# A decoder step's state-space mixer: value products of two attention steps in one run, the skip term on ScalarE, the decays' logs of a group loaded ahead

## The chip, the core and the metric

The kernel runs on one core of a Trainium2 chip. The metric is the time of one execution on the device in microseconds (us), the median of three runs. A profile of one execution is read beside it. TensorE (PE in the profile) does the matrix products, VectorE (DVE) and ScalarE (ACT) the elementwise work, GpSimd (POOL) some additions, and SyncE (SP) issues most transfers.

## What is computed

One layer of a hybrid decoder for 256 prompt positions and 8 sample rows of width 2048, all in float32. The part that matters here is the first sub-layer: one input projection, whose columns are split among a sliding-window attention (16 query heads, 4 key heads, window 128) and a Mamba-2 state-space mixer (32 heads in 4 groups, chunks of 128 positions).

```python
proj = rms_norm(x, w['g_mix']) @ w['w_in']
q, k, v, z, xbc, dt_raw = jnp.split(proj, IN_SPLITS, axis=-1)
# attention over the window: logits, softmax with a sink, then
o = jnp.einsum('bnkgqs,bnskd->bnqkgd', p.astype(v.dtype), vv)
# mixer, after a causal convolution and SiLU of x, B and C:
la = jnp.cumsum(dt * a, axis=2)                       # per head and chunk
decay = jnp.exp(jnp.where(causal, la[:, :, :, None] - la[:, :, None, :], -jnp.inf))
y = jnp.einsum('bclsgh,bcsghp->bclghp', cb[..., None] * decay, xdt)
y = y + jnp.einsum('bclgn,bcghpn->bclghp', cm, h_prev) * jnp.exp(la)[..., None]
y = y + xs * d_skip                                   # the skip term
y = rms_norm(y * silu(z), norm_g)
x = x + jnp.concatenate([attn, ssd], axis=-1) @ w['w_out']
```

Cross-attention and a convolutional feed-forward network follow. The sample rows take one step of the same formulas from states in memory: their y needs, for each head, the stored state h0 times C, summed.

## The kernel before

**Projections.** A weight arrives in parts of 128 x 1024 (`wraw`, line 83, SP's queue). ScalarE rounds it to a high half (`whi`, L89), VectorE makes the low half from the rest (`wlo`, L90), and TensorE multiplies: three matmuls for each 128x128 block (L104 to L106: high times high, high times low of the activations, low times high), 24 for a part, 264 columns each. There are four buffers each of wraw, whi and wlo. An input pair (`in_pair`) is four parts and ends in two accumulators that VectorE takes out of PSUM.

**The order of the work.** A scheduler sets each engine's order while the program is built; a name that stands in `tc.issue_after(...)` keeps an instruction behind another one, and weights have high priority. Each engine then runs its list strictly in order. So small matmuls of the attention and the mixer lie between the projections' matmuls where the scheduler put them.

**Attention.** `attn_first(j)` does the first 128 queries of two query blocks j and j+1, `attn_prompt(j, ..., 1)` the second 128 of one block: logits, softmax on VectorE and ScalarE, transposes of the probabilities into PSUM, a copy to `pt`, and then four value matmuls of 64 output rows each, L602 in the one and L564 in the other. The norms of q come from eight matmuls with 32 output rows (L620), two for each of four column groups. `attn_sample` does the sample rows.

**Mixer.** `la`, the cumulative logs, comes from a product with a triangle of ones (L479, L480); a turned copy of it is computed by two more matmuls (L482) and written to memory as `dram_la`. `ssd_prompt(g)` works on group g in two chunks: it loads the logs of four heads at a time, broadcast to all partitions, into tiles `e` (L810; three buffers shared with `kl` of the attention), turns them into decays (L814, L815 on ScalarE), multiplies with C times B (L816 on VectorE), multiplies with x dt on TensorE (L830, eight matmuls of 64 rows), and adds the skip term on VectorE, four instructions (L833). The carried state's part needs `ti`, loaded by L841. `ssd_sample(g)` loads half of the group's C rows (`cb`, L870, GpSimd's queue) and a quarter of a state (`h0`, L873), and VectorE multiplies and sums (L874, L875). `conv_pair` and `z_pair` take two accumulators out into separate tiles `u` of a ring of four.

The stage's order in the program is: `conv_group` 0 and 1, `ssd_prompt(0)`, `conv_group(2)`, `ssd_sample(0)`, `ssd_prompt(1)`, `conv_group(3)`, and then the z pairs with the other groups between them.

Of the kernel before, what the change touches and what calls it, by code (L numbers as in the profile page):

```python
# [7 lines left out]
F32 = mybir.dt.float32  # L8
F32R = mybir.dt.float32r
AF = mybir.ActivationFunctionType  # L10
ALU = mybir.AluOpType
# [37 lines left out]
def hybrid_decoder_step_kernel(ctx: ExitStack, tc: tile.TileContext, I, O):  # L49
# [26 lines left out]
    def weights(src, n=2048, into=None):  # L76

        out = []
        with tc.high_priority():
            for o in range(0, n, NPART):  # L80
                w = min(NPART, n - o)
                x = raw_part(w)
                nc.sync.dma_start(out=x, in_=src[:, o:o + w])
# [397 lines left out]
    for c in range(2):  # L481
        PE.matmul(p[0:32, 128 + c * 128:256 + c * 128], dtan[:, c, :], tri, start=True, stop=True)  # L482
# [11 lines left out]
    for i in range(4):  # L494
        u = mp.tile([128, 3 + T], F32, name=f"u{i}")
        P.memset(u[:, 0:3], 0.0)
        ring.append(u)
    ringn = [0]

    def next_u():  # L500
        ringn[0] += 1
        return ring[ringn[0] % 4]

    laT = next_u()[0:32, 3:259]
    V.tensor_copy(out=laT, in_=p[0:32, 128:384])
    nc.sync.dma_start(out=dram_la.rearrange("c h l -> h c l"), in_=laT.rearrange("p (c l) -> p c l", c=2))
# [18 lines left out]
    def attn_prompt(j, rq, nrq, c):  # L525
# [33 lines left out]
        pt = mp.tile([128, 4, 128], F32, tag="bc", name="pt", bufs=2)  # L559
        S.copy(out=pt[:, 0:2 * nb, :], in_=p[:, 0:2 * nk].rearrange("p (a q) -> p a q", q=128))  # L560
        o = psum("t")
        for h in range(2):
            for kb in range(nb):
                PE.matmul(o[64 * h:64 * h + 64, 0:128], vn[:, kb, pp, 64 * h:64 * h + 64], pt[:, h * nb + kb, :],  # L564
                          start=kb == 0, stop=kb == nb - 1)
        marks["attn"] = S.copy(out=attn[:, j, c * 128:c * 128 + 128], in_=o[:, 0:128])

    def attn_first(j):
# [29 lines left out]
        S.copy(out=pt, in_=p.rearrange("p (a q) -> p a q", q=128))  # L598
        o = psum("t")
        for i in range(4):  # L600
            h = i % 2
            PE.matmul(o[64 * h:64 * h + 64, 128 * (i // 2):128 * (i // 2) + 128], vn[:, 0, pp, 64 * h:64 * h + 64], pt[:, i, :], start=True, stop=True)  # L602
        S.copy(out=attn[:, j:j + 2, 0:128], in_=o[:, 0:256].rearrange("p (i q) -> p i q", i=2))
# [14 lines left out]
    for d in range(2):  # L618
        for j in range(4):
            PE.matmul(pq[32 * j:32 * j + 32, 0:TP], nw[:, d, :], qsq[d][:, j, :TP], start=d == 0, stop=d == 1)  # L620
# [42 lines left out]
    for j in range(0, 8, 2):  # L663
        attn_first(j)
# [934 lines left out]
```

## Time and profile before

| what | value |
|---|---|
| median of three runs | 1382.97 us (1382.23 to 1383.33) |
| the profiled execution | 1382.65 us, span 1380.6 us |
| TensorE busy | 1375.4 us, weight loads 1348.0 us |
| VectorE, ScalarE, GpSimd busy | 1050.0, 765.8, 96.1 us |
| L602, 16 matmuls in 32 records | 2.6 us busy |
| L564, 32 matmuls in 64 records | 5.3 us busy |
| L620, 8 matmuls in 16 records | 2.3 us busy |
| L482, 2 matmuls in 4 records | 0.6 us busy |
| L830, 64 matmuls in 128 records | 9.0 us busy |

A float32 matmul is two records in the profile, a projection's matmul and a transpose are one. Records of TensorE overlap, so what a matmul costs is read from start to start. The mixer and attention stage lies between about 40 and 410 us of the span; the projections go on through all of it.

### The profile page before, as it was taken

Reading aid. Unit: us, or ns where it says so; the run is one execution under the profiler, and the core shown is the slowest. Engines: PE = TensorE matmul, PEld = TensorE weight load, DVE = VectorE, ACT = ScalarE, POOL = GpSimd, SP = SyncE. Lnnn points to the kernel's source line nnn. Section 1 sums busy time; section 2 is a strip of 40 time slices with the busy share of each in tenths; the row PEclk is TensorE's granted clock in tenths of the full one; section 3 lists DMA queues with packets and bytes.
Section 4 is the critical chain, followed back from the end, with each engine's and each line's share of the span. In section 5 each row is a group of like instructions: output and inputs, shape, how many; then the busy total and the mean of one; then the engine's idle time right before and its main releaser. Section 6 shows DMA issues by size and latency. Waiting matters only on the chain.

```text
span 1380.6 us, 28767 instructions
## 1 busy us (share of the span) xinstructions
PE 1375.4 (100%) x11415; PEld 1348.0 (98%) x11415; DVE 1050.0 (76%) x1865; ACT 765.8 (55%) x1261; POOL 96.1 (7%) x286
## 2 busy tenths in 40 slices
PE   9999999999999999999999999999999999999999
PEld 8999999999999999899999999999999999999998
DVE  7979799999987784579777765776577657765655
ACT  7667756556545555566565544554455445543532
POOL 0000011111000000002010000000000000000000
PEclk9999999999999999999999999999999999999999
DMA  7954468777677576865676766676567656656554
GB/s 297 333 161 134 147 209 254 228 247 256 227 230 240 185 232 213 303 235 198 190 260 214 257 215 186 212 260 213 185 214 244 198 183 198 198 183 185 193 186 139
DMA packets 89478, 298.32 MB, mean 216 GB/s; under 512 B 12032, under 2 KB 17152, under 8 KB 88832
## 3 DMA queue, kind: packets, MB, share of 16 engines
q1 hardware_dynamic: 83840, 277.61, 60.5%
q0 software_dynamic: 5504, 18.88, 4.2%
q8 instruction: 89, 1.46, 0.4%
q14 instruction: 45, 0.37, 0.1%
HBM read 280.77 MB, written 16.23 MB: 215 GB/s over the span
## 4 chain that ended last, share of the span: by engine, by line
PE 99%; DMA 0%; ACT 0%; SPq 0%; DVE 0%; issue 0%
PE mm L106 21%; PE mm L104 21%; PE mm L105 21%; PE t L106 10%; PE t L104 10%; PE t L105 10%; PE t L245 1%; PE t L283 1%; PE y L830 1%; PE y L846 0%; PE x L283 0%; DMA open<-in_open_dram 0%; PE s L245 0%; PE mm L245 0%; PE t L564 0%; PE x L1144 0%
## 5 line engine op out<-in xcount | busy, mean ns | idle before, releaser
L89 ACT CAST whi<-wraw 128x1024 fp32r<-128x1024 f32 x440 | 459.9, 1047 | 518.3 <-PE mm L105 270.2
L90 DVE TENSOR_TENSOR wlo<-wraw,whi 128x1024 fp32r<-128x1024 f32 x440 | 541.7, 1232 | 216.4 <-ACT whi L89 210.2
L106 PE MATMUL t<-x2h,wlo 128*128 128x264 f32 x704 | 198.5, 282 | 0.0
L104 PE MATMUL t<-x2h,whi 128*128 128x264 f32 x704 | 198.4, 282 | 0.0
L105 PE MATMUL t<-x2l,whi 128*128 128x264 f32 x704 | 198.4, 282 | 0.0
L105 PE MATMUL mm<-hl,whi 128*128 128x264 f32 x704 | 197.5, 282 | 0.0
L106 PE MATMUL mm<-hh,wlo 128*128 128x264 f32 x704 | 197.2, 282 | 0.0
L104 PE MATMUL mm<-hh,whi 128*128 128x264 f32 x704 | 195.7, 282 | 0.0
L104 PE MATMUL mm<-x2h,whi 128*128 128x264 f32 x672 | 189.3, 282 | 0.0
L105 PE MATMUL mm<-x2l,whi 128*128 128x264 f32 x672 | 189.3, 282 | 0.0
L106 PE MATMUL mm<-x2h,wlo 128*128 128x264 f32 x672 | 189.3, 282 | 0.0
L104 PE MATMUL mm<-xh,whi 128*128 128x264 f32 x576 | 163.7, 285 | 0.0
L105 PE MATMUL mm<-xl,whi 128*128 128x264 f32 x576 | 163.4, 285 | 0.0
L106 PE MATMUL mm<-xh,wlo 128*128 128x264 f32 x576 | 162.3, 286 | 0.0
L104 PEld LDWEIGHTS t<-x2h,whi 128*128 128x128 f32 x704 | 131.9, 187 | 0.0
L106 PEld LDWEIGHTS t<-x2h,wlo 128*128 128x128 f32 x704 | 131.9, 187 | 0.0
L105 PEld LDWEIGHTS t<-x2l,whi 128*128 128x128 f32 x704 | 131.9, 187 | 0.0
L105 PEld LDWEIGHTS mm<-hl,whi 128*128 128x128 f32 x704 | 131.9, 187 | 0.0
L106 PEld LDWEIGHTS mm<-hh,wlo 128*128 128x128 f32 x704 | 131.7, 187 | 0.0
L104 PEld LDWEIGHTS mm<-hh,whi 128*128 128x128 f32 x704 | 130.8, 187 | 0.0
L104 PEld LDWEIGHTS mm<-x2h,whi 128*128 128x128 f32 x672 | 125.9, 187 | 0.0
L105 PEld LDWEIGHTS mm<-x2l,whi 128*128 128x128 f32 x672 | 125.9, 187 | 0.0
(518 smaller groups left out, 2939.5 us busy)
## 6 DMA issues: line engine op xcount, KB each, us to landing
wraw<-in_w_up_dram SPq DMA_DIRECT2D x176, 512.0 KB, 4.2
wraw<-in_w_in_dram SPq DMA_DIRECT2D x96, 512.0 KB, 4.7
wraw<-in_w_dn_dram SPq DMA_DIRECT2D x88, 512.0 KB, 4.3
wraw<-in_w_out_dram SPq DMA_DIRECT2D x48, 512.0 KB, 4.3
h<-in_h_dram POOLq DMA_DIRECT2D x32, 256.0 KB, 4.6
hn<-in_h_dram SPq DMA_DIRECT2D x16, 512.0 KB, 4.9
out_state_s_dram<-hn POOLq DMA_DIRECT2D x16, 512.0 KB, 3.5
e<-dram_la SPq DMA_DIRECT2D x16, 256.0 KB, 4.4
```

The source lines that it names most:

```text
L89: S.copy(out=hi, in_=x)
L90: V.tensor_tensor(out=lo, in0=x, in1=hi.bitcast(F32), op=ALU.subtract)
L104: PE.matmul(out, wh, xh, start=start, stop=False)
L105: PE.matmul(out, wh, xl, start=False, stop=False)
L106: return PE.matmul(out, wl, xh, start=False, stop=stop)
L245: PE.matmul(first[c][:, :T], pre[k // 2][i][:, k % 2, c * 128:(c + 1) * 128], A[k // 8][x][:, k % 8, :], start=k + i + x == 0, stop=k == K ...
L283: return PE.transpose(out, in_, cst[0:k, C_ID:C_ID + k])
L830: PE.matmul(y[o:o + 64, (h // 2) * 128:(h // 2) * 128 + 128], xdt[:, h, :], es[h // 4][:, h % 4, :], start=True, stop=True)
```

## The change

Seven edits, all in the mixer and attention stage.

1. The value matmuls of two steps are issued in one run: `first_values` and `second_values` take the probabilities of two steps, the newer one's first matmul goes first, and the others are held behind it. Their copy out of PSUM is one instruction for both. A second pair of tiles for `pt` comes from the tags `hp` and `cb`.
2. The eight q-norm matmuls go in one run, behind the one whose input comes last.
3. The turned logs are one transpose of `la`, and `dram_la` is written from 64 rows.
4. The logs of a whole group (both chunks and `ti`) are loaded by `logs()` into one tile `late` with the tag `B`, that is, into the buffers that the attention's tiles (keys, values, zeros) had; the first two groups' loads stand ahead of `conv_group(1)`, the others behind a weight load. The product with C times B is one instruction for eight heads.
5. The skip term: ScalarE scales x by d_skip in place, four instructions, and VectorE adds y in one.
6. Pairs: `conv_pair` and `z_pair` use one tile `u` for both accumulators, so that copies, the tanh and the products of z are one instruction for two.
7. `ssd_sample` loads the group's C rows in one transfer; `ssd_sample(0)` stands ahead of `conv_group(1)`. Two small tiles of `attn_sample` move from the tag `h0` to `hp`.

```diff
-    for c in range(2):
-        PE.matmul(p[0:32, 128 + c * 128:256 + c * 128], dtan[:, c, :], tri, start=True, stop=True)
...
-    for i in range(4):
-        u = mp.tile([128, 3 + T], F32, name=f"u{i}")
+    for i in range(2):
+        u = mp.tile([128, 2, 3 + T], F32, name=f"u{i}")
...
+    p = psum("x")
+    tr(p[0:64, 0:128], la)
+    V.tensor_copy(out=laT, in_=p[0:64, 0:128])
+    nc.sync.dma_start(out=dram_la.rearrange("c h l -> (c h) l"), in_=laT)
...
-        o = psum("t")
-        for h in range(2):
-            for kb in range(nb):
-                PE.matmul(o[64 * h:64 * h + 64, 0:128], vn[:, kb, pp, 64 * h:64 * h + 64], pt[:, h * nb + kb, :],
-                          start=kb == 0, stop=kb == nb - 1)
-        marks["attn"] = S.copy(out=attn[:, j, c * 128:c * 128 + 128], in_=o[:, 0:128])
+        return pt
+
+    def second_values(j, pts):
+        pp = j // 4
+        o = psum("t")
+
+        def value(a, h, kb):
+            return PE.matmul(o[64 * h:64 * h + 64, 128 * a:128 * a + 128], vn[:, kb, pp, 64 * h:64 * h + 64], pts[a][:, 2 * h + kb, :],
+                             start=kb == 0, stop=kb == 1)
+
+        with tc.issue_after(value(1, 0, 0).ins):
+            for x in [(a, h, kb) for a in (1, 0) for h in range(2) for kb in range(2)][1:]:
+                value(*x)
+        marks["attn"] = S.copy(out=attn[:, j:j + 2, 128:TP], in_=o[:, 0:256].rearrange("p (i q) -> p i q", i=2))
...
-    for d in range(2):
-        for j in range(4):
-            PE.matmul(pq[32 * j:32 * j + 32, 0:TP], nw[:, d, :], qsq[d][:, j, :TP], start=d == 0, stop=d == 1)
+    with tc.issue_after(q_sums(1, 3).ins):
+        for d in (1, 0):
+            for j in range(4):
+                if (d, j) != (1, 3):
+                    q_sums(d, j)
...
+    def logs():
+
+        g = len(lates)
+        w = apool.tile([128, 8 * PITCH], F32, tag="B", name="late", bufs=4)
+        for c in range(2):
+            nc.sync.dma_start(out=w[:, 1024 * c:1024 * c + 1024].rearrange("p (h l) -> p h l", h=8),
+                              in_=dram_la[c, 8 * g:8 * g + 8, :].partition_broadcast(128))
+        ti = w[:, 2048:2560].rearrange("p (i l) -> p i l", i=4)
+        for h in range(2):
+            nc.sync.dma_start(out=ti[h * 64:h * 64 + 64], in_=lav[h][4 * g:4 * g + 4, :].partition_broadcast(64))
+        lates.append(w)
...
-            for i in range(4):
-                V.scalar_tensor_tensor(out=x[:, i, :], in0=x[:, i, :], scalar=pc("d_skip", 4 * g + i), in1=y[:, i * 128:i * 128 + 128],
-                                       op0=ALU.mult, op1=ALU.add)
+            for i in range(4):
+                S.activation(out=x[:, i, :], in_=x[:, i, :], func=AF.Copy, scale=pc("d_skip", 4 * g + i))
+            V.tensor_tensor(out=x, in0=x, in1=y.rearrange("p (i l) -> p i l", i=4), op=ALU.add)
...
+        cb = mp.tile([128, 8, 128], F32, tag="cb", name="cb", bufs=1)
+        nc.gpsimd.dma_start(out=cb, in_=dram_bc[1][8 * g:8 * g + 8, :].partition_broadcast(128))
...
     conv_group(0)
+    ssd_sample(0)
+    logs()
+    logs()
     conv_group(1)
     ssd_prompt(0)
     conv_group(2)
-    ssd_sample(0)
+    with tc.issue_after(marks["load"].ins):
+        logs()
     ssd_prompt(1)
     conv_group(3)
+    with tc.issue_after(marks["load"].ins):
+        logs()
```

Three places show how the engines' lists change. On TensorE, where the logs are made and q's squares are summed, it was (L104 to L106 are projections, L620 the sums):

```order
L104 MATMUL mm<-xh_77,whi 128x264
L479 MATMUL x<-dtan,cst 128x64
L480 MATMUL x<-dtan,cst 128x64
L482 MATMUL x<-cst,dtan 32x128 x2
L105 MATMUL mm<-xl_78,whi 128x264
L106 MATMUL mm<-xh_77,wlo 128x264
L104 MATMUL mm<-xh_77,whi 128x264
L105 MATMUL mm<-xl_78,whi 128x264
L106 MATMUL mm<-xh_77,wlo 128x264
L620 MATMUL s<-qsq_677,zz 32x256 x4
L620 MATMUL s<-qsq_678,zz 32x256 x2
```

and later two lone matmuls of L620. Now L479 and L480 stand alone, and some 36 projections later comes this (L637 is the new line of the sums):

```order
L106 MATMUL mm<-xh_75,wlo 128x264
L104 MATMUL mm<-xh_75,whi 128x264
L283 MATMUL x<-cst,la 64x128
L105 MATMUL mm<-xl_76,whi 128x264
L637 MATMUL s<-qsq_674,zz 32x256 x4
L637 MATMUL s<-qsq_673,zz 32x256 x4
```

The eight sums are one run, and the transpose of la has taken the place of L482. The value matmuls, also on TensorE, at the first of their runs, before and then in the change:

```order
L105 MATMUL mm<-xl_78,whi 128x264
L106 MATMUL mm<-xh_77,wlo 128x264
L602 MATMUL t<-pt,vn 64x128 x4
L104 MATMUL mm<-xh_77,whi 128x264
L105 MATMUL mm<-xl_78,whi 128x264
```

```order
L105 MATMUL mm<-xl_76,whi 128x264
L106 MATMUL mm<-xh_75,wlo 128x264
L104 MATMUL mm<-xh_75,whi 128x264
L615 MATMUL t<-pt,vn 64x128 x8
L105 MATMUL mm<-xl_76,whi 128x264
```

Twelve such runs of four are now six runs of eight. On VectorE, at the start of the attention's sample rows (qs_sq and sts are theirs, h and cb belong to `ssd_sample`), before and now:

```order
L685 COPY zz<-qs_sq 64x2x4x4 x4
L90 TENSOR_TENSOR wlo<-wraw,whi 128x1024
L752 SCALAR_TENSOR_TENSOR xs_2163<-xs_2163,c 128x2x256
L695 TENSOR_REDUCE sts<-s 128x1
L696 TENSOR_TENSOR sts<-sts,par 128x1
L697 TENSOR_SCALAR sts<-sts 128x1
L90 TENSOR_TENSOR wlo<-wraw,whi 128x1024
```

```order
L709 COPY zz<-qs_sq 64x2x4x4 x4
L90 TENSOR_TENSOR wlo<-wraw,whi 128x1024
L773 SCALAR_TENSOR_TENSOR xs_2142<-xs_2142,c 128x2x256
L901 TENSOR_TENSOR h_2440<-h_2440,cb 128x512
L901 TENSOR_TENSOR h_2444<-h_2444,cb 128x512
L901 TENSOR_TENSOR h_2448<-h_2448,cb 128x512
L902 TENSOR_REDUCE ych<-h_2440 128x4
L90 TENSOR_TENSOR wlo<-wraw,whi 128x1024
```

The sample rows' products with the state, which began four weight parts later before, stand ahead of the low half there.

More of the change, by code (lines that the diff above doesn't have):

```diff
@@ L82, in weights @@
                 x = raw_part(w)
-                nc.sync.dma_start(out=x, in_=src[:, o:o + w])
+                marks["load"] = nc.sync.dma_start(out=x, in_=src[:, o:o + w])
                 if into:
@@ L501, in next_u @@
         ringn[0] += 1
[L502 to L506, printed above, removed]
+        return ring[ringn[0] % 2]
+    laT = next_u()[0:64, 0, 3:131]
+    p = psum("x")
+    tr(p[0:64, 0:128], la)
+    V.tensor_copy(out=laT, in_=p[0:64, 0:128])
+    nc.sync.dma_start(out=dram_la.rearrange("c h l -> (c h) l"), in_=laT)
     dsm = mp.tile([32, 2, 8], F32, name="dsm")
@@ L598, in attn_first, with first_values, value @@
         S.copy(out=pt, in_=p.rearrange("p (a q) -> p a q", q=128))
+        return pt
+    def first_values(pp, pts):
         o = psum("t")
-        for i in range(4):
+        def value(a, i):
             h = i % 2
-            PE.matmul(o[64 * h:64 * h + 64, 128 * (i // 2):128 * (i // 2) + 128], vn[:, 0, pp, 64 * h:64 * h + 64], pt[:, i, :], start=True, stop=True)
-        S.copy(out=attn[:, j:j + 2, 0:128], in_=o[:, 0:256].rearrange("p (i q) -> p i q", i=2))
+            c = 256 * a + 128 * (i // 2)
+            return PE.matmul(o[64 * h:64 * h + 64, c:c + 128], vn[:, 0, pp, 64 * h:64 * h + 64], pts[a][:, i, :], start=True, stop=True)
+        with tc.issue_after(value(1, 0).ins):
+            for a, i in [(a, i) for a in (1, 0) for i in range(4)][1:]:
+                value(a, i)
+        S.copy(out=attn[:, 4 * pp:4 * pp + 4, 0:128], in_=o.rearrange("p (i q) -> p i q", i=4))
     qsq = [T3(apool, 4, tag="R", name=f"qsq{i}", bufs=4) for i in range(2)]
@@ L645, in hybrid_decoder_step_kernel @@
     kh = [mp.tile([128, 2, TP], F32R, tag="xdt", name="kh", bufs=2) for _ in range(2)]
-    kl = [mp.tile([128, 2, TP], F32R, tag="e", name="kl", bufs=3) for _ in range(2)]
+    kl = [mp.tile([128, 2, TP], F32R, tag="e", name="kl", bufs=2) for _ in range(2)]
     qs = [apool.tile([128, 4, 2, 128], F32R, tag="R", name=f"qs{i}", bufs=4) for i in range(2)]
@@ L661, in second_chunk @@
             V.tensor_tensor(out=qs[pp][ho, :, h, :], in0=x, in1=hi.bitcast(F32), op=ALU.subtract)
+    for pp in range(2):
+        first_values(pp, [attn_first(4 * pp + 2 * a) for a in range(2)])
     for j in range(0, 8, 2):
-        attn_first(j)
-    for j in range(8):
         if j % 4 == 0:
@@ L698, in attn_sample @@
         S.activation(out=es, in_=sk, func=AF.Exp, bias=mx)
-        e = mp.tile([128, 129], F32, tag="h0", name="es_e", bufs=3)
+        own = mp.tile([128, 512], F32, tag="hp", name="own", bufs=1)
+        e = own[:, 0:129]
         S.activation(out=e, in_=p[:, 0:129], func=AF.Exp, bias=mx, accum_out=den)
@@ L706, in attn_sample @@
         V.tensor_copy(out=zdiag(1)[:, :, :, 0:8], in_=p[:, 0:128].rearrange("p (j t c) -> p t j c", j=4, c=8))
-        dg = mp.tile([128, 128], F32, tag="h0", name="dgs", bufs=3)
+        dg = own[:, 256:384]
         V.tensor_scalar(out=dg, in0=ident, scalar1=e[:, 128:129], scalar2=None, op0=ALU.mult)
@@ L838, in ssd_prompt @@
                     PE.matmul(yi[:, i * 128:i * 128 + 128], hp[:, i * 128:i * 128 + 128], CT[:, g, cs], start=True, stop=True)
-                ti = mp.tile([128, 4, 128], F32, tag="bc", name="ti", bufs=2)
-                for h in range(2):
-                    nc.sync.dma_start(out=ti[h * 64:h * 64 + 64], in_=lav[h][4 * g:4 * g + 4, :].partition_broadcast(64))
+                ti = late[:, 2048:2560].rearrange("p (i l) -> p i l", i=4)
                 S.activation(out=ti, in_=ti, func=AF.Exp)
```

72 lines of the change are left out of this document (32 added, 40 removed).

## The prediction

> **What bounds the kernel now.** I read the page's busy shares first, then the chain of work that ended last, the view of waits for TensorE, and TensorE's timeline where the matmul stream is interrupted.
>
> ```profile
> span 1380.6 us, 28767 instructions
> PE 1375.4 (100%) x11415; PEld 1348.0 (98%) x11415; DVE 1050.0 (76%) x1865; ACT 765.8 (55%) x1261; POOL 96.1 (7%) x286
> PE 99%; DMA 0%; ACT 0%; SPq 0%; DVE 0%; issue 0%
> ```
>
> TensorE holds 99% of the chain, and the view of its waits from 40 us to the end has no row: it never waits for anything. A faster VectorE, ScalarE or transfer therefore buys nothing by itself. Only what shortens TensorE's own stream counts, and only what makes it wait costs. The stream is projections, one matmul each 0.12 us, with short runs of other matmuls in between. The price of such a run is the time from the last projection before it to the second one behind it, less two steps of 0.12, since the first projection behind a run takes 0.2 us instead of 0.12:
>
> ```profile
> 107.33 0.28 PE L106 MATMUL mm<-xh,wlo 128*128 128x264 f32 x1
> 107.54 0.66 PE L602 MATMUL t<-pt,vn 128*64 128x128 f32 x8
> ...
> 108.35 0.28 PE L105 MATMUL mm<-xl,whi 128*128 128x264 f32 x1
> 228.26 0.28 PE L106 MATMUL t<-xh,wlo 128*128 128x264 f32 x1
> 228.47 1.09 PE L830 MATMUL y<-e,xdt 128*64 128x128 f32 x16
> ...
> 229.72 0.28 PE L105 MATMUL t<-xl,whi 128*128 128x264 f32 x1
> ```
>
> Four 64-column matmuls (eight records, two for each) cost 1.02 - 0.24 = 0.78 us; eight in one run cost 1.46 - 0.24 = 1.22. So two runs of four put together save 2 x 0.78 - 1.22 = 0.34 us, the fixed price of a break in the stream.
>
> The second thing to read is how near VectorE, which makes the low half of every weight part, is to being the bound in the state-space stage:
>
> ```profile
> 150.00:190.00 40.00, 40.00 (x388) 38.16 (x387) 30.71 (x80) 28.95 (x56) 2.33 (x4) 1.00 0.52 163
> 190.00:260.00 70.00, 70.00 (x590) 68.28 (x590) 69.87 (x136) 37.57 (x60) 14.71 (x19) 1.00 0.73 234
> 260.00:330.00 70.00, 70.00 (x595) 67.45 (x594) 70.00 (x142) 42.84 (x81) 10.01 (x13) 1.00 0.77 247
> ```
>
> The columns are the stretch, its length, then TensorE, weight load, VectorE, ScalarE. From 190 to 330 us VectorE is busy 139.87 of 140 us. It keeps up, but with no reserve; ScalarE has 27 to 32 us free in each 70. In the 40 us ahead of that VectorE idles 9.3 us.
>
> **The change part by part: TensorE.** *Value runs.* Twelve runs of four (L602 four times, L564 eight times) become six of eight (L615, L568). Six times 0.34 is 2.04 us. More of the old runs than of the new stand directly against transposes and share a break with them, so I round down: **1.9 us**. Least, if pairs that accumulate gain a fourth less than the L830 row: 1.5.
>
> *Sums of squares of q.* The eight matmuls stood in three runs, and now in one (L637).
>
> ```profile
> 81.00 0.28 PE L106 MATMUL mm<-xh,wlo 128*128 128x264 f32 x1
> 81.21 1.06 PE L620 MATMUL s<-qsq,zz 128*32 128x256 f32 x12
> ...
> 82.44 0.29 PE L105 MATMUL mm<-xl,whi 128*128 128x264 f32 x1
> 83.17 0.28 PE L105 MATMUL mm<-xl,whi 128*128 128x264 f32 x1
> 83.38 0.62 PE L620 MATMUL s<-qsq,zz 128*32 128x256 f32 x2
> ...
> 84.16 0.28 PE L104 MATMUL mm<-xh,whi 128*128 128x264 f32 x1
> ...
> 85.93 0.62 PE L620 MATMUL s<-qsq,zz 128*32 128x256 f32 x2
> ```
>
> Six of them cost 1.44 - 0.24 = 1.20 us, one alone 0.99 - 0.24 = 0.75, and the other lone one (85.93) the same. Four 32-column matmuls lie side by side, so the last two of eight join the second round that the run of six already pays: 1.22 for the new run. Saved 1.20 + 2 x 0.75 - 1.22 = **1.5 us**. If the two added ones ran on their own behind the others, at the 0.62 us of a lone one, the new run would cost 1.20 + 1.24 = 2.44, and 0.3 be saved: the least.
>
> *Cumulative logs turned.* Two 32-row matmuls (L482) become one transpose of la, 64 columns.
>
> ```profile
> 79.25 0.28 PE L104 MATMUL mm<-xh,whi 128*128 128x264 f32 x1
> 79.37 0.33 PE L479 MATMUL x<-dtan,cst 128*128 128x64 f32 x2
> ...
> 79.85 0.62 PE L482 MATMUL x<-cst,dtan 128*32 128x128 f32 x4
> ...
> 80.63 0.29 PE L106 MATMUL mm<-xh,wlo 128*128 128x264 f32 x1
> ...
> 154.93 0.28 PE L105 MATMUL mm<-xl,whi 128*128 128x264 f32 x1
> 155.05 0.27 PE L283 MATMUL x<-cst,bcs 128*32 128x128 f32 x1
> ...
> 155.28 0.28 PE L104 MATMUL mm<-xh,whi 128*128 128x264 f32 x1
> ```
>
> The old run costs 1.38 - 0.24 = 1.14 us; L479 and L480 alone keep about 0.45 of it (0.48 from the first's start to L482's). The narrow transpose of bcs costs 0.35 - 0.24 = 0.11. Saved 0.69 - 0.11 = **0.6 us**; least, if la's transpose cost as much as a lone narrow run, nothing. The Trainium skill (TensorEngine Tiling (Array Packing), Key Properties) says that changing the tiling mode drains TensorE. If a transpose into 64 rows were such a change, this term would be nothing and the sum 0.6 us later; the bcs row, a transpose into 32 rows at 0.11, speaks against it.
>
> *The last chunk.* Its eight products per head stood in two runs, since the decays lay in two tiles; now one tile gives one run, **0.3 us**.
>
> ```profile
> 369.58 0.66 PE L830 MATMUL y<-e,xdt 128*64 128x128 f32 x8
> 373.73 0.66 PE L830 MATMUL y<-e,xdt 128*64 128x128 f32 x8
> ```
>
> Sum 1.9 + 1.5 + 0.6 + 0.3 = **4.3 us**, between 2.1 (1.5 + 0.3 + 0 + 0.3) and 4.7 (2.04, all of q's two breaks and of L482, 0.34).
>
> **The change part by part: VectorE, ScalarE and queues.** The skip term turns four 128x128 instructions on VectorE into one of 128x512, the pairs halve the small copies, and z's and the decays' products are fewer and wider.
>
> ```profile
> L833 DVE SCALAR_TENSOR_TENSOR xs<-xs,par,y 128x128 f32<-128x128 f32 x20 | 5.6, 344 | 0.0
> L896 DVE COPY zsam<-u 128x8 f32<-128x8 f32 x8 | 1.3, 166 | 0.0
> 178.91 1.22 DVE L90 TENSOR_TENSOR wlo<-wraw,whi 128x1024 fp32r<-128x1024 f32 x1
> 180.05 0.15 DVE L701 TENSOR_TENSOR sts<-sts 128x1 f32<-128x1 f32 x1
> 170.10 2.44 ACT L814 ACTIVATE e<-e,la 128x128 f32<-128x128 f32 x8
> ```
>
> VectorE starts an instruction 0.08 us before the one ahead has ended (180.05 against 180.13), so a removed copy of 0.17 is worth 0.08. By such steps 32 skip instructions give 32 x 0.26 - 8 x 0.60 = 3.5 us (0.60 for 512 columns from the pair of L874 below, 1.29 less the overlap), 20 copies 1.7, the products some more: about 6 us of VectorE, worth nothing while TensorE doesn't wait. The 32 new scalings on ScalarE, of the size of the L814 row (2.44 / 8 = 0.3), are 10 us in its free time.
>
> What moves matters more. The order puts the sample work (h times C, and its sum) of the first two groups earlier:
>
> ```profile
> 202.83 1.29 DVE L874 TENSOR_TENSOR h<-h,cb 128x512 f32<-128x512 f32 x2
> 204.04 1.22 DVE L90 TENSOR_TENSOR wlo<-wraw,whi 128x1024 fp32r<-128x1024 f32 x1
> 208.94 0.28 PE L104 MATMUL mm<-xh,whi 128*128 128x264 f32 x1
> ```
>
> The low half that is done at 205.3 is the 51st of its line, and its first matmul, counted in parts of 24, starts at 208.94: 3.7 us of lead. In the new order 13 more of these instructions, at 0.60 from start to start, and three that prepare the first chunk, stand ahead of the same low half: 7.8 + 1.4 = 9.2 us. TensorE also wants it 4.0 us earlier. Against 13.2 stand 3.7 of lead and the 9.3 that VectorE idled from 150 to 190: short by 0.2 if all of that idle time can be filled. Some can't: of it
>
> ```profile
> 170.23 0.55 DVE L288 RECIPROCAL qs_sq<-qs_sq 128x64 f32<-128x64 f32 x1 [2.37 <-ACT qs_sq L287]
> 173.51 1.23 DVE L90 TENSOR_TENSOR wlo<-wraw,whi 128x1024 fp32r<-128x1024 f32 x1 [1.71 <-ACT whi L89]
> ```
>
> both gaps come from ScalarE, which did the logs of the first chunk in just that place (the L814 row); in the new order they stand three parts later and will make a gap there. I take **0.5 us** of waiting, with 0 and 5 (half of the idle time lost) as ends. The Trainium skill (VectorE: DVE Perf Modes, The DRAIN you can't avoid) says that the next VectorE operation doesn't start until the pipe is empty; by it the 13 cost 0.68 each, 1 us more, and the wait would be 1.5. The row at 180.05, a start ahead of the end, speaks against it.
>
> The C rows in one transfer and the earlier cb change nothing on the path.
>
> **The rivals.** *A: VectorE becomes the bound.* If half or more of the idle time can't be filled, TensorE waits 2 to 5 us and the gain is mostly given back: 1382.97 - 4.3 + 3 = 1381.7. For it: 139.87 of 140. Against it: VectorE's own 6 us less, which arrives by the end of the stage.
>
> *B: slower.* The logs of a group, 1.3 MB, go out together on SP's queue, each into a tile that the attention must have left, and the weights behind them wait.
>
> ```profile
> e<-dram_la SPq DMA_DIRECT2D x16, 256.0 KB, 4.4
> ```
>
> At the 234 GB/s of the windows 1.3 MB take 5.6 us; with a lead of 2 us each of four groups would cost 3.6: 1382.97 - 4.3 + 14.4 = 1393.1. It decides as soon as the delay exceeds the lead by 1.8 us for each group. Against it: the same bytes go through the same queue now, in transfers of 256 KB, and a weight part is asked for four parts (12 us) ahead.
>
> *C: the breaks stay.* If a run of eight costs as much as two of four, only q's sums and the logs are left: 1382.97 - 2.1 = 1380.9. The L830 row speaks against it.
>
> **How the numbers follow.** The profiled execution took 1382.65 us, 2.05 around its span, and lies 0.3 below the median of 1382.97. From 1382.65 the sum makes 1378.3, with 0.5 of waiting 1378.8; told from the median, **1379.2**. Chances: this forecast (0 to 1.5 us of waiting) 0.62, A 0.24, B 0.07, C 0.07. A measurement of this kernel can tell about 0.2% (2.8 us) from no change, so faster means below 1380.2: the forecast nearly whole and some of A, 0.65; same 0.27; slower 0.08. The range 1378.0 to 1382.4 leaves out B and the worst of A.
>
> **What would show it.** Right: runs of 16 records on L615 and L568 at 1.22 us, one L637 run near 1.22, la's transpose at 0.11, and no waits of TensorE between 180 and 260 us. Wrong: a row of TensorE's waits that names wlo (A) or wraw's transfer through whi (B), with gaps of more than 0.12 us between projections there; or L615 runs of 1.5 us (C).

## The result and the profile after

| | before | changed |
|---|---|---|
| median, 22 runs each | 1382.72 us | 1385.11 us |
| lowest | 1381.88 us | 1383.15 us |
| ratio to before | 1 | 1.0018 (1.0012 to 1.0024) |
| the profiled execution, its span | 1382.65, 1380.6 us | 1384.6, 1382.6 us |

The change made the kernel 0.18% slower, 2.4 us. One of the changed kernel's 22 runs took 1927.39 us at a granted clock of 0.655, and the ratio leaves it out. 1379.2 was forecast: the sign was wrong, and the time lies 2.7 us above the top of the range. The prediction took 0.2% as the least that can be told from no change; this is just below it, but the interval of the ratio leaves 1 out. The page of the changed kernel, its span, busy shares and the chain that ended last:

```profile
span 1382.6 us, 28660 instructions
PE 1373.3 (99%) x11412; PEld 1348.3 (98%) x11412; DVE 1043.6 (75%) x1797; ACT 772.8 (56%) x1271; POOL 89.4 (6%) x280
PE 94%; DVE 3%; DMA 1%; issue 1%; ACT 0%; POOL 0%; SPq 0%; DVEq 0%; POOLq 0%; ACTq 0%
```

TensorE is busy 2.1 us less than before (1375.4), and yet the span is 2.0 us longer: VectorE now has 3% of the chain, where it had none. First, the savings. TensorE's timeline at q's sums (with la's transpose just ahead) and at the first merged value run:

```profile
84.31 0.28 PE L104 MATMUL mm<-xh,whi 128*128 128x264 f32 x1
84.44 0.27 PE L283 MATMUL x<-cst,la 128*64 128x128 f32 x1
84.46 0.37 PE L105 MATMUL mm<-xl,whi 128*128 128x264 f32 x1
84.76 1.07 PE L637 MATMUL s<-qsq,zz 128*32 128x256 f32 x16
...
85.99 0.28 PE L104 MATMUL mm<-xh,whi 128*128 128x264 f32 x1
...
110.48 0.28 PE L104 MATMUL mm<-xh,whi 128*128 128x264 f32 x1
110.69 1.09 PE L615 MATMUL t<-pt,vn 128*64 128x128 f32 x16
...
111.94 0.28 PE L106 MATMUL mm<-xh,wlo 128*128 128x264 f32 x1
```

The value run of eight costs 1.46 - 0.24 = 1.22 us, as forecast. La's transpose and q's run together cost 1.68 - 3 x 0.12 = 1.32; 0.11 + 1.22 = 1.33 was forecast. Counted by projections, the 1153rd one of the whole kernel started at 177.80 us before and starts at 174.07 now; the 73rd stood at 14.25 and 14.68. So between 14 and 178 us the changed kernel gained 3.73 + 0.43 = 4.2 us, all that the forecast had for that stretch (4.3 without the last chunk's 0.3 is 4.0).

Then it loses them. TensorE's waits (waited for, total us, times, longest) have a row that was not there before, and the stretches show where:

```profile
PE mm L106 <- DVE wlo L90: 3.6, 4, 2.0
```

```profile
150.00:190.00 40.00, 38.03 (x338) 36.73 (x336) 31.02 (x74) 28.16 (x56) 6.43 (x12) 0.96 0.66 212
190.00:260.00 70.00, 68.41 (x591) 65.92 (x590) 68.96 (x125) 54.51 (x110) 9.77 (x16) 1.00 0.83 271
260.00:330.00 70.00, 70.00 (x595) 67.31 (x594) 70.00 (x118) 34.78 (x57) 8.21 (x13) 1.00 0.71 225
```

TensorE was busy through all of them before; now it misses 2.0 us in the first and 1.6 in the second. The longest wait is for the low half of the 44th weight part. Followed back, ScalarE, VectorE and TensorE in turn:

```profile
171.31 1.05 ACT L89 CAST whi<-wraw 128x1024 fp32r<-128x1024 f32 x1 [2.60 <-issue]
175.40 4.80 ACT L844 ACTIVATE late<-late,la 128x128 f32<-128x128 f32 x16 [3.03 <-DMA late<-dram_la]
...
180.63 1.04 ACT L89 CAST whi<-wraw 128x1024 fp32r<-128x1024 f32 x1
```

```profile
179.59 0.69 DVE L901 TENSOR_TENSOR h<-h,cb 128x512 f32<-128x512 f32 x1 [4.19 <-DMA h<-in_h_dram]
...
182.41 0.69 DVE L901 TENSOR_TENSOR h<-h,cb 128x512 f32<-128x512 f32 x1
183.02 0.68 DVE L902 TENSOR_REDUCE ych<-h 128x4 f32<-128x512 f32 x1
183.62 0.15 DVE L727 RECIPROCAL sts<-sts 128x1 f32<-128x1 f32 x1
183.69 0.67 DVE L902 TENSOR_REDUCE ych<-h 128x4 f32<-128x512 f32 x1
184.27 1.22 DVE L90 TENSOR_TENSOR wlo<-wraw,whi 128x1024 fp32r<-128x1024 f32 x1
```

```profile
183.07 0.28 PE L105 MATMUL mm<-xl,whi 128*128 128x264 f32 x1
183.19 0.38 PE L283 MATMUL x<-cst,xs 128*128 128x128 f32 x2
185.54 0.39 PE L106 MATMUL mm<-xh,wlo 128*128 128x264 f32 x1 [1.97 <-DVE wlo L90]
```

ScalarE reaches the decays' scalings, waits 3.0 us for the late logs, works 4.8 us on all 16, and only then casts the next weight part: 9.3 us between two casts. VectorE in turn waits 4.2 us for a state, and when the high half is there (181.7), one product of the sample rows has just begun and three more products and sums of theirs still stand ahead of the low half, which is done at 185.5. And the wait has a tail, as the windows behind it show (TensorE, weight load, VectorE, ScalarE, GpSimd, then the granted clock):

```profile
185.50:187.00 1.50, 1.46 (x7) 1.46 (x8) 1.50 (x5) 1.50 (x3) 0.00 (x0) 0.62 0.86 309
187.00:189.30 2.30, 2.30 (x12) 2.30 (x12) 2.30 (x8) 1.61 (x4) 0.53 (x1) 0.51 0.63 223
```

TensorE's granted clock is halved for 3.4 us, from 185.9 to 189.3; 15 matmuls take 0.22 us each instead of 0.12, 1.5 us more. Waits 3.6, the low clock 1.5, and, as an estimate, 0.1 for each of four restarts (the first projection behind a run takes 0.2 instead of 0.12) make 5.5 us lost against 4.2 and 0.3 gained: about 1.0 of the 2.0 us. The later start of the 73rd projection is 0.4 more; 0.6 is left over in small steps.

### The profile page after: what moved, and what is told of

Read it like the earlier page. It is cut to its first block, busy times and chain, and to the rows that moved or that the text cites. A ratio compares the mean times of both kernels' runs of the same rounds, so it can differ in the third digit from the quotient of the medians.

```text
span 1382.6 us, 28660 instructions
## 1 busy us (share of the span) xinstructions
PE 1373.3 (99%) x11412; PEld 1348.3 (98%) x11412; DVE 1043.6 (75%) x1797; ACT 772.8 (56%) x1271; POOL 89.4 (6%) x280
## 3 DMA queue, kind: packets, MB, share of 16 engines
q8 instruction: 89, 1.46, 0.4%
## 4 chain that ended last, share of the span: by engine, by line
PE 94%; DVE 3%; DMA 1%; issue 1%; ACT 0%; POOL 0%; SPq 0%; DVEq 0%; POOLq 0%; ACTq 0%
PE mm L106 20%; PE mm L104 19%; PE mm L105 19%; PE t L106 9%; PE t L104 9%; PE t L105 9%; DMA h<-in_h_dram 1%; DVE wlo L90 1%; PE t L245 1%; PE t L283 1%; PE y L859 1%; PE y L873 0%; DVE h L901 0%; DMA open<-in_open_dram 0%; DVE ych L902 0%
## 5 line engine op out<-in xcount | busy, mean ns | idle before, releaser
L89 ACT CAST whi<-wraw 128x1024 fp32r<-128x1024 f32 x440 | 459.9, 1048 | 525.0 <-PE mm L105 259.8
L90 DVE TENSOR_TENSOR wlo<-wraw,whi 128x1024 fp32r<-128x1024 f32 x440 | 541.8, 1233 | 221.2 <-ACT whi L89 215.4
L106 PE MATMUL t<-x2h,wlo 128*128 128x264 f32 x704 | 198.6, 282 | 0.0
L104 PE MATMUL t<-x2h,whi 128*128 128x264 f32 x704 | 198.4, 282 | 0.0
L106 PE MATMUL mm<-hh,wlo 128*128 128x264 f32 x704 | 197.2, 282 | 0.0
L104 PE MATMUL mm<-hh,whi 128*128 128x264 f32 x704 | 195.7, 282 | 0.0
L104 PE MATMUL mm<-x2h,whi 128*128 128x264 f32 x672 | 189.4, 282 | 0.0
L106 PE MATMUL mm<-x2h,wlo 128*128 128x264 f32 x672 | 189.4, 282 | 0.0
L106 PE MATMUL mm<-xh,wlo 128*128 128x264 f32 x576 | 161.9, 288 | 3.6 <-DVE wlo L90 3.6
L104 PE MATMUL mm<-xh,whi 128*128 128x264 f32 x576 | 163.7, 286 | 0.0
L104 PEld LDWEIGHTS t<-x2h,whi 128*128 128x128 f32 x704 | 131.9, 187 | 0.0
L106 PEld LDWEIGHTS t<-x2h,wlo 128*128 128x128 f32 x704 | 131.9, 187 | 0.0
L106 PEld LDWEIGHTS mm<-hh,wlo 128*128 128x128 f32 x704 | 131.6, 187 | 0.0
L104 PEld LDWEIGHTS mm<-hh,whi 128*128 128x128 f32 x704 | 130.8, 187 | 0.0
L104 PEld LDWEIGHTS mm<-x2h,whi 128*128 128x128 f32 x672 | 125.9, 187 | 0.0
```

The lines of the kernel that those rows point to most:

```text
L89: S.copy(out=hi, in_=x)
L90: V.tensor_tensor(out=lo, in0=x, in1=hi.bitcast(F32), op=ALU.subtract)
L104: PE.matmul(out, wh, xh, start=start, stop=False)
L106: return PE.matmul(out, wl, xh, start=False, stop=stop)
```

## The experiments

Two theories stood at first. **L**: the late logs hold ScalarE, so the high halves are late. **D**: VectorE is the bound, because products of the sample rows with C (L901, L902) stand ahead of low halves: in the changed kernel's order they begin behind 41 low halves and end behind 86, before the change behind 45 and 105. In the traces VectorE is busy 7.3, 7.7 and 6.0 us longer than before between the start of the 37th low half and the start of the 45th, 51st and 65th (the expectations sum rows' durations over the order and get 8.0, 8.4 and 4.9; they number parts and these halves from 0, so their part 43 is the 44th). All runs were timed in five rounds, each against the kernel before on the same chip. A trace is of one execution, which in e2, e3, e4, e7 and e13 lies over 1 us from the median (1385.37, 1382.19, 1387.53, 1382.40 and 1385.00 us), so the waits named below are of that execution. In e3 to e7, e14 and e15 `ssd_sample(0)` also stands at its old place again, behind `conv_group(2)`, which the shortened diffs below don't show.

| run | edit | median us | ratio to before |
|---|---|---|---|
| e1 | decays' logs and C rows loaded as before | 1384.92 | 1.0019 (1.0010 to 1.0028) |
| e2 | first group's scalings behind later casts | 1384.06 | 1.0009 (1.0000 to 1.0018) |
| e3 | first group's products behind the 46th low half | 1383.23 | 1.0006 (0.9998 to 1.0015) |
| e4 | e2 and e3 | 1383.94 | 1.0012 (1.0003 to 1.0021) |
| e5 | all products paced | 1379.38 | 0.9976 (0.9967 to 0.9985) |
| e6 | e5 and e2 | 1380.55 | 0.9989 (0.9980 to 0.9998) |
| e7 | e5, q's sums as before | 1384.20 | 1.0010 (1.0001 to 1.0019) |
| e8 | kernel before, products paced | 1386.48 | 1.0027 (1.0017 to 1.0037) |
| e9 | sample attention's tiles as before | 1385.09 | 1.0018 (1.0009 to 1.0027) |
| e10 | kernel before, only those tiles moved | 1388.48 | 1.0044 (1.0031 to 1.0056) |
| e11 | sums cut to 8 columns | 1385.26 | 1.0018 (1.0009 to 1.0027) |
| e12 | states not loaded | 1385.90 | 1.0023 (1.0014 to 1.0032) |
| e13 | e11 and e12 | 1386.73 | 1.0028 (1.0016 to 1.0039) |
| e14 | e5 and e1 | 1380.01 | 0.9980 (0.9971 to 0.9989) |
| e15 | first group's products paced only | 1381.25 | 0.9988 (0.9980 to 0.9997) |

### e1 to e4: moving one thing

e1, from the changed kernel (it undoes edit 4 and the transfer of the C rows of edit 7, the fifth and sixth parts of the expectation):

```diff
-            e = late[:, 1024 * c:1024 * c + 1024].rearrange("p (h l) -> p h l", h=8)
...
+            for hh in range(2):
+                e = mp.tile([128, 4, 128], F32, tag="e", name="e", bufs=3)
...
+                nc.sync.dma_start(out=e, in_=dram_la[c, h0:h0 + 4, :].partition_broadcast(128))
...
-                ti = late[:, 2048:2560].rearrange("p (i l) -> p i l", i=4)
+                ti = mp.tile([128, 4, 128], F32, tag="bc", name="ti", bufs=2)
```

> The changed kernel with its fifth and sixth parts undone: the decays' logs are loaded again in pieces of 256 KB into the mixer's own tiles, ti and the C rows as before; pairs, the long value runs, q's sums, la's transpose and the skip term on ScalarE stay. In its order the first 12 scalings of the decays stand behind 40 weight casts, as before the change, but the sample products on VectorE still begin at the 41st low half, as in the changed kernel. Theory L (the late logs: ScalarE waits 3.0 us for them and then works 4.8 us on 16 scalings ahead of the cast of part 43, which TensorE wants): no wait of TensorE near 183 us, about 4 us less than before: 1378.5 to 1379.5. Theory D (rival A of the prediction: VectorE is the bound, because the sample products stand ahead of the low halves): the waits stay, 1381.5 to 1385.

Measured 1384.92. L falls as the sole cause: the first group's logs are there when ScalarE comes to them (12 scalings from 162.6 us on, without a wait for logs), and the loss is whole. The later groups' logs are not early: one more wait of TensorE, at 278 us, is for a high half that ScalarE casts behind a wait of 5.5 us for logs. TensorE's longest wait comes one part later than in the changed kernel (the first two rows, its waits), and VectorE's products now wait for the C rows (the last row; the last two are of all waits from 165 to 345 us):

```profile
PE mm L106 <- DVE wlo L90: 2.6, 3, 1.5
PE mm L104 <- ACT whi L89: 1.5, 1, 1.5
...
ACT e L835 <- DMA e<-dram_la: 15.3, 6, 5.5
...
DVE h L895 <- DMA cb<-dram_bc: 4.3, 2, 2.7
```

e2 (casts and lows are lists of the L89 and L90 instructions, counted from 0):

```diff
-            with tc.issue_after(marks["attn"].ins):
+            with tc.issue_after(casts[(44, 47)[c]].ins if g == 0 else marks["attn"].ins):
```

> The changed kernel with one order added: the scalings and the exponent of the first group's decays stand on ScalarE behind the 45th weight cast (first half) and the 48th (second half) instead of ahead of the 44th. Loads, tiles and everything else stay. Theory L: the wait of 2 us for the low half of part 43 goes, and with it the stretch at the lower clock: 1378.5 to 1380.5. Theory D: the sample products still stand ahead (6 of them up to the 45th low half instead of 8), the waits stay within 1 us: 1383 to 1385.

Measured 1384.06, 1 us better than the changed kernel, but in D's range. The wait at the 44th part goes, and another takes its place, for a transpose whose input waits in VectorE's queue behind the state that isn't there yet:

```profile
PE t L283 <- DVE csm L779: 2.2, 1, 2.2
```

e3:

```diff
-                V.tensor_tensor(out=h0, in0=h0, in1=cb[:, rows, :], op=ALU.mult)
+                with tc.issue_after(lows[45 if g == 0 else 0].ins): V.tensor_tensor(out=h0, in0=h0, in1=cb[:, rows, :], op=ALU.mult)
```

> The changed kernel with one order added on VectorE: the products of the first group's state with C (sample rows) stand behind the 46th low half instead of the 41st. The scheduler then also puts 8 of the first 16 scalings of the decays behind the 44th cast on ScalarE instead of ahead of it. Theory L: ScalarE still waits 3 us for the logs, but works 2.4 us on them instead of 4.8: the wait at part 43 shrinks from 2 us to about 0 to 1, 1380.5 to 1383.5. Theory D: VectorE is 4 us or more ahead at each low half from the 42nd to the 46th, no waits: 1378.5 to 1380.

Measured 1383.23, in L's range and 3 us above D's. The eight products no longer stand ahead of the 44th part, but six of them now stand together behind the 46th to 48th low half, and two waits of 0.8 and 1.4 us follow at 203 and 206 us.

e4 has both edits.

> Both orders added: the first group's decays on ScalarE behind the 45th weight cast and the sample products on VectorE behind the 46th low half. Theories L and D alike: no wait of TensorE between 180 and 200 us, 1378 to 1380; if it is over 1382, neither is the cause, or the waits only move to the stretch from 205 to 265 us, where VectorE has no idle time.

Measured 1383.94: no better than e3. The expectation left two readings for a time over 1382, that neither theory holds or that the waits only move; e5 speaks for the second. Its longest wait comes at 263 us from another list again:

```profile
PE y L859 <- ACT hp L875: 2.6, 1, 2.6
```

### e5 to e8: the products spread out

e5 gives each of the 32 products a place of its own, one behind every 1.8th low half:

```diff
+                with tc.issue_after(lows[min(int(46 + 1.8 * (8 * g + 4 * q + i)), len(lows) - 1)].ins): V.tensor_tensor(out=h0, in0=h0, in1=cb[:, rows, :], op=ALU.mult)
```

> The changed kernel with one order added on VectorE: the 32 products of the state with C stand one by one behind the 47th low half, then every 1.8th (46 + 1.8 n), up to the 102nd; the changed kernel has them between the 41st and the 86th, the one before between the 45th and the 105th. Loads, tiles, TensorE's work and ScalarE's logs stay. Summed by the rows' durations, VectorE's work ahead of the 44th, 50th and 64th low half is 8.0, 8.4 and 4.9 us more than before in the changed kernel, and 0.0, -3.6 and -5.6 us here. Theory D (VectorE is the bound, since work that is not urgent stands ahead of the low halves): no waits for low halves from 190 us on, 1378.3 to 1379.8. Theory L (the logs' 3.0 us on ScalarE): 8 scalings still stand ahead of the 44th cast, so a wait near 183 us stays: 1380.5 to 1382.5.

Measured 1379.38: 5.7 us better than the changed kernel, 3.3 us better than before, as D expected. It is the version that beats both. ScalarE, then VectorE at the place where the changed kernel stalled; TensorE's waits; and the stretch behind it:

```profile
175.03 2.45 ACT L844 ACTIVATE late<-late,la 128x128 f32<-128x128 f32 x8 [2.81 <-DMA late<-dram_la]
...
183.40 1.05 ACT L89 CAST whi<-wraw 128x1024 fp32r<-128x1024 f32 x1
```

```profile
178.45 1.23 DVE L90 TENSOR_TENSOR wlo<-wraw,whi 128x1024 fp32r<-128x1024 f32 x1 [3.00 <-ACT whi L89]
...
184.48 1.23 DVE L90 TENSOR_TENSOR wlo<-wraw,whi 128x1024 fp32r<-128x1024 f32 x1 [0.45 <-ACT whi L89]
```

```profile
PE mm L106 <- DVE wlo L90: 0.3, 1, 0.3
```

```profile
190.00:260.00 70.00, 69.71 (x583) 66.89 (x582) 67.57 (x115) 54.85 (x106) 8.43 (x13) 1.00 0.78 242
```

ScalarE still waits 2.8 us for the logs. But VectorE now waits for ScalarE instead of the reverse: the low half starts as soon as the high half is there, and that is early enough.

e6 adds e2's line to it.

> As the paced kernel, and the first group's scalings on ScalarE stand behind the 45th and 48th weight casts. Theory D: 1378.3 to 1380, the same as the paced one within 0.5. Theory L: this one alone is near 1379, and 1.5 to 3 us faster than the paced one.

Measured 1380.55, a miss for both: not better than e5, and not the same, but 1.2 us worse, with one wait of 1.4 us for the same copy of hp as in e4. Taking the logs out of the casts' way is worth nothing once the products are spread.

e7 undoes q's run in e5:

```diff
-    with tc.issue_after(q_sums(1, 3).ins):
-        for d in (1, 0):
...
+    for d in range(2):
+        for j in range(4):
+            PE.matmul(pq[32 * j:32 * j + 32, 0:TP], nw[:, d, :], qsq[d][:, j, :TP], start=d == 0, stop=d == 1)
```

> As the paced kernel, with one edit of the change undone: q's sums are written as before, so that the scheduler parts them again into several runs. If a saved run break is worth its price wherever TensorE doesn't wait: 1.5 us slower than the paced kernel, 1379.8 to 1381.3. If TensorE's savings don't count because VectorE sets the end of the stage: the same as the paced kernel within 0.5.

Measured 1384.20, 4.8 us slower than e5, more than either expected. Between the 73rd and the 1153rd projection e7 gains 2.64 us on the kernel before, e5 4.02, so the run is worth its 1.4 us there; but the small edit made the scheduler write another order, with waits of 1.9 and 1.0 us. A saved break is real, and whether it arrives is decided by the order behind it. The products' places are those of e5, so they alone don't make a fast kernel; other work of VectorE came forward (see behind e15).

e8 paces the kernel before in the same way.

> The kernel before the change with the same pace for its 32 state products (behind low halves 46 + 1.8 n). It has no waits of TensorE there, so by both theories pacing is worth nothing here: 1382.2 to 1383.2. Should it be over 1 us faster, the pace does something else than take waits away.

Measured 1386.48, 3.8 us slower. At 404 us it is level with the kernel before (0.3 us ahead). Then the last product, behind 107 low halves instead of 105, makes the sample rows' tail late:

```profile
PE y L300 <- DVE accy L923: 2.6, 1, 2.6
```

Pacing by itself gives nothing here; and VectorE's list is full to the end (0.01 us idle between the 91st and the 111th low half), so too late costs as too early does.

### e9 and e10: what drew the products forward

The earlier place of `ssd_sample(0)` in the program draws them forward by one part at most: e9 keeps it, and there they begin behind the 44th low half, against the 45th before. What draws them further is the last edit of the change: the sample attention's two small tiles no longer take buffers of `h0`, so the states' loads need not wait for that attention. e9 undoes it in the changed kernel, e10 makes it alone in the kernel before:

```diff
-        e = mp.tile([128, 129], F32, tag="h0", name="es_e", bufs=3)
+        own = mp.tile([128, 512], F32, tag="hp", name="own", bufs=1); e = own[:, 0:129]
...
-        dg = mp.tile([128, 128], F32, tag="h0", name="dgs", bufs=3)
+        dg = own[:, 256:384]
```

> The changed kernel with one small edit undone: the sample attention's weights and their diagonal lie again in two of the three tiles of the state (tag h0), as before the change, instead of in a tile of their own. The state's first load then waits again for that attention, and by the order VectorE's 32 products with C begin behind the 44th low half instead of the 41st; its work ahead of the 44th, 50th and 64th low half is 2.3, 3.8 and 1.5 us more than before instead of 8.0, 8.4 and 4.9. Theory D: part of the loss comes back, waits of 0 to 2 us in all: 1380 to 1383. Theory L (late logs): 8 of the 16 scalings still stand ahead of the 44th cast and wait 3 us: 1381.5 to 1383.5. If the edit doesn't matter: 1384 to 1386.

Measured 1385.09: a miss for D and L, the edit makes no difference to the time there. The products begin three parts later, but eight crowd behind the 44th to 48th low half, and waits come at 191, 202 and 204 us.

> The kernel before the change with only that edit made: the sample attention's weights and diagonal in a tile of their own (tag hp). The state's loads no longer wait for them, the products with C begin behind the 39th low half instead of the 45th, and VectorE's work ahead of low halves 44 to 86 is 4 to 8 us more than before. TensorE's work and the logs' loads stay as they were. Theory D: waits for low halves although TensorE is no faster, 1384 to 1388. Theory L: nothing changes, 1382.2 to 1383.2.

Measured 1388.48, 5.7 us slower than the kernel before, by an edit that touches neither TensorE's matmuls nor the logs' loads. That is the clearest run for the place of the products, which begin behind the 39th low half. TensorE's waits in it sum up to 3.5 us, and the rest of the loss isn't traced. VectorE and two rows of these waits:

```profile
167.57 1.29 DVE L874 TENSOR_TENSOR h<-h,cb 128x512 f32<-128x512 f32 x2 [2.45 <-DMA cb<-dram_bc]
```

```profile
PE mm L106 <- DVE wlo L90: 1.1, 2, 0.9
PE t L106 <- DVE wlo L90: 0.8, 1, 0.8
```

### e11 to e13: is it the amount?

e11 cuts the 32 sums to 8 of 128 columns (the first two lines); e12 lets the products read the identity matrix and leaves the states' loads out (the last three); e13 does both.

```diff
-                V.tensor_reduce(out=ych[:, 4 * g + i, rows], in_=h0, op=ALU.add, axis=AX.X)
+                V.tensor_reduce(out=ych[:, 4 * g + i, rows], in_=h0[:, :, 0:8], op=ALU.add, axis=AX.X)
...
-                nc.gpsimd.dma_start(out=h0, in_=I["h0"][4 * g + i][:, rows, :])
-                V.tensor_tensor(out=h0, in0=h0, in1=cb[:, rows, :], op=ALU.mult)
...
+                V.tensor_tensor(out=h0, in0=ident.unsqueeze(1).broadcast_to([128, 4, 128]), in1=cb[:, rows, :], op=ALU.mult)
```

> The changed kernel with the 32 sums over the state's products cut to 8 of 128 columns (the rest of these sums is left out, so the sample rows' state term is not the whole one). The logs' loads and the 16 scalings ahead of the 44th cast stay, and the products stand where they stood; VectorE has about 32 x 0.5 = 16 us less to do in the stage. Theory D: the waits nearly vanish, at most 1 us left at part 43, 1378.3 to 1380. Theory L: the wait of 2 us with the low clock behind it stays, 1381.5 to 1384.

Measured 1385.26: D, as it was put (too much work), falls. With 14.8 us less on VectorE two waits above 2 us remain. One comes behind a product that waits 5.2 us for its state. The other is for the 49th low half: its cast stands behind the second group's scalings, which had waited 3.8 us for their logs, and the low half then stands behind VectorE's other work for 1.9 us more.

> The changed kernel in which the 32 products with C read the resident identity matrix in place of the state, and the state's 32 loads for them are left out (so the sample rows' state term is not computed); VectorE has the same 32 products and 32 sums to do, 8 of them again ahead of the 44th low half and 3 more ahead of the 45th. If VectorE's wait for these loads (4.2 us at 175 us in the changed kernel) is what makes the low halves late: 1378.5 to 1380.5. If it is the amount of work ahead of the low halves: 1383 to 1387. If it is ScalarE behind the late logs: 1382.5 to 1385.5, with the wait at the 44th part.

Measured 1385.90, in the range for the amount of work ahead of the low halves; the total amount is refuted by e11 and e13. The loss doesn't need VectorE's waits for the states. What these waits cost in the changed kernel the run doesn't tell, since its order puts 11 products ahead of the 45th low half instead of 8.

> As the one without the state's loads, and the 32 sums cut to 8 of 128 columns (left out beside the loads: most of these sums). VectorE then has neither the loads to wait for nor 16 us of its work; the late logs and the 16 scalings ahead of the 44th cast on ScalarE stay. If VectorE's queue is the cause, by work or by waits: 1378.3 to 1380. If the late logs on ScalarE alone hold TensorE up: 1381.5 to 1384.

Measured 1386.73, the second worst of all, with the least work for VectorE; even L's range is exceeded. With nothing to wait for, the scheduler drew the products further forward: six now stand between the 44th and the 45th low half, two in the changed kernel. ScalarE, VectorE and TensorE there:

```profile
184.46 3.89 ACT L89 CAST whi<-wraw 128x1024 fp32r<-128x1024 f32 x4
```

```profile
188.25 1.22 DVE L90 TENSOR_TENSOR wlo<-wraw,whi 128x1024 fp32r<-128x1024 f32 x1
```

```profile
189.53 0.51 PE L106 MATMUL mm<-xh,wlo 128*128 128x264 f32 x1 [3.15 <-DVE wlo L90]
```

The high half is ready at 185.5, the low half starts at 188.25, behind six products. From the 56th part on the low halves are mostly 2 to 9 us ahead of their use, and it helps no more.

### e14 and e15: the fourth corner, and the place

> The fourth corner: the paced order of VectorE's state products, and the decays' logs loaded as before the change in pieces of 256 KB into the mixer's tiles (with the C rows in halves). If the place of the products is the cause and the logs' loads are not: like the paced kernel, 1378.8 to 1380.5. If the late logs have a share of their own that pacing only covers: up to 1 us faster than the paced kernel. If the products' place isn't the cause: 1383 to 1386.

Measured 1380.01. With it the four corners are: products early, logs late 1385.11; products early, logs as before 1384.92; products paced, logs late 1379.38; products paced, logs as before 1380.01. Spreading the products is worth 5.7 and 4.9 us, the logs' loads -0.2 and +0.6. Nor do ScalarE's waits for logs go with the time. From 40 to 420 us they are longer in the kernel before than in the changed one, and longest in e14 (in this order):

```profile
ACT e L814 <- DMA e<-dram_la: 13.2, 6, 4.7
ACT late L844 <- DMA late<-dram_la: 9.5, 5, 3.2
ACT e L835 <- DMA e<-dram_la: 17.9, 7, 4.6
```

e15 paces the first group only (behind low halves 46 + 1.3 n):

```diff
+                with tc.issue_after(lows[min(int(46 + 1.3 * (4 * q + i)), len(lows) - 1) if g == 0 else 0].ins): V.tensor_tensor(out=h0, in0=h0, in1=cb[:, rows, :], op=ALU.mult)
```

> The changed kernel with only the first group's 8 products paced, behind the 47th low half and then every 1.3th; the other 24 stand where the scheduler puts them (59th to 98th). If what counts is the stretch of parts 43 to 52, where the leads are shortest: like the paced kernel, 1379 to 1380.5. If VectorE is tight in the whole stage: waits from part 59 on, 1381 to 1383.5.

Measured 1381.25: 3.9 of the 5.7 us come from the first group, and the rest is lost later, most at 297 us (1.0 us). So the stretch around the 44th to 52nd part holds up to two thirds of it (the other 24 products moved too, from the 48th to 86th low half to the 59th to 98th), and VectorE is tight beyond it.

One number separates the fast kernels from the slow ones: VectorE's busy time between the start of the 37th and the start of the 51st low half. Before, changed, and e5:

```profile
152.17:204.04 51.87, 42.52 (x102) 1.00 0.55 178
150.10:209.96 59.86, 50.19 (x113) 0.97 0.76 247
149.99:202.85 52.86, 40.43 (x93) 1.00 0.70 214
```

Against the kernel before it is -3.7 us in e14, -2.1 in e5, -0.9 in e15 and +1.0 in e6, the four that are faster. It is +2.0 to +7.7 in all that are slower, with +2.0 in e7, +2.3 in e13, +2.8 in e11 and +4.5 in e9, but for e8 (-2.3), which loses its time at 415 us. It doesn't rank the slower ones among themselves, and it is one trace of each.

## Why the prediction was wrong

**What bounds the kernel: right** for the kernel before. The chain and the waits said that only TensorE's stream counts, and e5 shows it: as soon as TensorE hardly waits (0.3 us), 3.3 us of the forecast 4.3 arrive; where the last 1.0 stays isn't traced.

**TensorE's part, 4.3 us: right**, term by term. The merged value run that stands alone cost the forecast 1.22 us, la and q together 1.32 against 1.33, and 4.2 us were gained by 178 us against 4.0. The last chunk's one run cost 1.23, where its two had cost 0.78 each. (The upper end of the sum is 2.04 + 1.5 + 0.69 + 0.34 = 4.6 by its own terms, not 4.7.) The rule of the Trainium skill that was weighed there (TensorEngine Tiling (Array Packing), Key Properties: a changed mode drains) did not show in la's transpose: it lies inside those 1.32 us.

**VectorE's part, 0.5 us of waiting: this step failed.** TensorE waited 3.6 us in four waits, all for low halves. The working had the right stretch and nearly the right quantity: 13.2 us wanted against 3.7 of lead and 9.3 of idle time, "short by 0.2 if all of that idle time can be filled"; of the 9.2 us of work in it, 7.7 show ahead of the 51st low half. But it looked at that one half, and the longest wait came at the 44th. Three more things went wrong.
- The idle time could not be filled. Between the 37th and the 44th low half VectorE idled 8.6 us before and 8.9 now, although 4.6 us of work were added there. The text itself said that the gaps come from ScalarE's logs and would move with them; it then took 0.5 us all the same. The end of its range, "5 (half of the idle time lost)", was the better value.
- The work drawn forward brought waits of its own: a product waits 4.2 us for its state, and the list behind it stands still. The prediction summed durations, and asked of no moved instruction whether its input would be there.
- A wait was priced at its length. The longest one cost 1.5 us more by the halved clock.

**Rival A** (1381.7) had the sign of the mechanism and was 3.4 us short. Its price, waits of 2 to 5 us, was met by the waits alone (3.6); the clock, the restarts and the later start are the rest. Its name, that VectorE becomes the bound, is too simple: e11 and e13 took 15 us of work from VectorE and gained nothing, e5 took none and gained 5.7. What counts is what stands ahead of the halves in lists that are worked off strictly in order.

**Rival B** (late logs) cost nothing like its 14.4 us. The delay of the 44th part came on another engine than told, in ScalarE's list, by 3.0 us of waiting and 4.8 of work; e1 and e14 show that it decides nothing by itself. The casts do wait longer for the weights' transfers than before (from 40 to 420 us, before and changed):

```profile
ACT whi L89 <- DMA wraw<-in_w_in_dram: 5.5, 5, 1.8
ACT whi L89 <- DMA wraw<-in_w_in_dram: 13.0, 7, 2.6
```

But no wait of TensorE in the changed kernel names a high half, and e15 has 18.6 us of such waits of the casts at 1381.25 us, so they don't decide it either.

**Rival C** is refuted by the 1.22 us of the new run.

The Trainium skill (VectorE: DVE Perf Modes, The DRAIN you can't avoid) would have put the wait at 1.5 us; the same section lets an operation that is not held start earlier. The traces after agree with the start some 0.08 us ahead of the end that the prediction used (184.27 against 183.69 + 0.67 = 184.36), so that was not what was missing.

**Open.** How much of each loss falls to the scalings and how much to the products could not be split cleanly, since every edit let the scheduler write another order. e7 and e9 show it: with the products' places of e5, or with products that begin three parts later, they are about as slow as the kernels with early products (1384.20 and 1385.09). VectorE's busy time ahead of the 51st low half fits both, but no run changes that time alone.

## What to carry to other kernels

A gain on the engine that bounds is only worth the lead that its suppliers still have: read the lead part by part (half ready against half used) before adding up savings. In lists that run in order, work that is not urgent belongs spread behind the urgent work, one piece at a time, not wherever its inputs are first ready; a freed buffer can be the edit that draws it forward. When many small edits each give another order, compare orders, not only edits.

## What the runs showed of the hardware

Around some of TensorE's waits the granted clock falls to about a half, in each of seven traces for 3.4 us. It did so behind waits of 1.97 us (the changed kernel), 2.19 (e2), 2.6 (e4, e8) and 3.15 us (e13), and also at two shorter waits close together: 0.56 and 1.41 us, 2.0 us apart, in e9, and 1.60 and 1.14 us, 1.4 us apart, in e12. It did not behind 1.94 (e7), nor behind 2.03 and 2.83 us in e11. The clock is the number behind the five engines' columns, or alone behind TensorE's; e13 first, then e11 and e9:

```profile
189.60:191.60 2.00, 2.00 (x10) 0.51 0.48 119
```

```profile
180.75:182.75 2.00, 2.00 (x17) 1.00 0.53 166
```

```profile
203.65:207.05 3.40, 3.28 (x16) 0.50 0.86 294
```

The Trainium skill (TensorE: Matmul & The Clock Gate, Part 1: The HAM clock gate) tells of a half clock after an idle window of about 3.4 us that runs freely; its section Why this matters for your kernels advises against gaps above about 3 us. A free window would fit that the length alone doesn't decide here, and 3.4 us is how long the clock stayed low; but in the changed kernel a gap of 1.97 us sufficed, and in e9 two that sum up to as much, which is shorter than the page allows for. In the changed kernel a wait of 2.0 us cost 3.5.
